# A hybrid decoder layer on one Trainium2 core: small loads moved behind weights and inputs, and GpSimd's work in the dilated attention put in another order

## The chip, the cores and the metric

The kernel runs on one core of one Trainium2 chip. The metric is the device time of one execution in microseconds (us). A core has a matrix engine (TensorE; PE in the profile, its weight loads PEld), VectorE (DVE), ScalarE (ACT), GpSimd (POOL) and SyncE (SP), each with an instruction queue of its own that it works off in order, and 16 DMA engines that move what the queues of SyncE and ScalarE issue.

## The reference, cut to what matters

```python
def hybrid_layer(x, ...):                       # x: 1 x 2048 x 1024, float32
    h = rmsnorm(x, norm_gain)
    proj = h @ w_in                             # 1024 x 2976 columns
    q_a, k_a, v_a, z_a, c_q, c_kv, k_rope, z_b = split(proj)
    # A: 8 heads of 64; three banded patterns (window 128/512/2048, dilation 1/4/16),
    #    mixed by their softmax denominators
    o_a = dilated_window_attention(rmsnorm(q_a), rmsnorm(k_a), v_a, rel_bias)
    # B: 8 heads, low-rank q and kv, rotary key, full causal attention
    o_b = latent_attention(c_q, c_kv, k_rope, positions, ...)
    mixed = concat([o_a * silu(z_a), o_b * silu(z_b)])
    return x + mixed @ w_out
```

## The kernel before, in words

All matrix products that need float32 accuracy are made as three products of two-part operands (`mm3`, line 230: a high part, rounded, and the rest).

**Stage 1, projections (about 0 to 600 us).** The x tiles (128 rows, 512 KB) are loaded by `x_load` (line 194) into three buffers, their square sums are taken (`h0`), they are scaled (`h1`), turned by TensorE and split (`h2`). The weights come in quarters of a column group: `w_load` (line 246) issues two DMAs into one of two buffers `wraw`, `w_split` (line 257) makes the two parts on ScalarE or GpSimd and on VectorE, and at its end issues the load of the quarter after the next one. Column groups run in the order g0, g1, q0, z0, ...; each for the first 8 tiles of rows, then again for the other 8. At the head of the stage (lines 278 to 310) stand, in the text: x tile 0, the norm's gain, a constant matrix CM, two quarters of weights, x tiles 1 and 2, then 14 small loads (positions, the rotary frequencies, gains; each 0.2 to 16 KB), then the splits. `rope_tables` (line 314) needs positions and frequencies; the units of group g1 need its tables and the gain of the rotary key; `up_weights` needs `ugain`; the column gains `gcol` are first used by the units of q0. In this stage the text does not fix the order on an engine: the program is built with `schedule_with_timeline_sim=True` (line 1742), and a scheduler orders the instructions of each queue when the program is built, by a simulation of its own.

**Stage 2, dilated attention (about 600 to 1000 us).** Here the order on every engine is that of the text (`tc.manual_schedule`, line 1544). The loop over `n` (line 1546) goes through 64 units, 8 for each head h (n = 8h + i). In one turn it issues the scores of a head ahead (`groups`: tiles on TensorE, reductions on VectorE, and `q_turn`, GpSimd's casts of Q), the exponentials of the next unit (ScalarE), the transposes and copies of this unit, then the products with V of the unit before (`p_pv`). One third of the third pattern's exponentials is made in one piece: GpSimd subtracts the maximum (line 997), ScalarE takes the exponential (998), VectorE sums (999).

When a head's units are through, its tail follows (`tail`, line 1242): a table from a step (counted from n = 8h + 8) to functions. `a_den0` makes two products on GpSimd (E8 and E32, lines 930 and 937) that TensorE reads in `a_den1` (line 1094), one step later; from them comes the reciprocal of the denominators, which goes through DRAM and comes back broadcast (`a_rd1`). `a_shift` loads the lower half of the accumulator (`bot`) and the gate (`gA_`). `a_sum` (line 1134, GpSimd) adds the halves, `a_gate` (line 1129, VectorE) multiplies gate and reciprocal, `a_out` (line 1139, GpSimd) multiplies both, `a_store` stores. Heads 6 and 7 use `a_outt` (line 1230), with no trip through DRAM. In a turn, step 1 runs ahead of `p_pv`; the other steps are put off behind it:

```python
                    for f in tail(g).get(n - 8 * g - 8, ()):
                        if n - 8 * g - 8 == 1:
                            f()
                        else:
                            late.append(f)
```

From n = 52 on, the loop also does the first pieces of the latent attention (`early`): loads and splits of its keys and queries (`b_split`, lines 1352 and 1353, on GpSimd) and its first scores.

**Stage 3, latent attention (about 1000 to 1340 us), and stage 4, the output product**, follow. The change does not touch their text.

Of the kernel before, what the change touches and what calls it, by code (L numbers as in the profile page):

```python
# [43 lines left out]
B3 = (1,)  # L44
# [57 lines left out]
def hybrid_kernel(ctx: ExitStack, tc: tile.TileContext, x, positions, rel_bias, norm_gain, w_in,  # L102
# [181 lines left out]
    x_load(2)  # L284

    pos_i = P1.tile([NB, 128], I32, name="pos_i")
    sp.dma_start(pos_i, positions.rearrange("o (b p) -> (o b) p", p=128))
    invf = P1.tile([128, 16], F32, name="invf")
    sp.dma_start(invf, bcast_rows(cinv, 16))
    gains = {}  # L290
    for nm, ap, n in (("qr", qr_gain, 32), ("kr", kr_gain, 32)):
        gains[nm] = P1.tile([128, n], F32, name="g_" + nm)
        sp.dma_start(gains[nm], bcast_rows(ap, n))
    ugain = P1.tile([128, 3], F32, name="ugain")
    sp.dma_start(ugain[:, 0:2], q_c_gain.rearrange("o (k p) -> p (o k)", p=128))
    sp.dma_start(ugain[:, 2:3], kv_c_gain.rearrange("o (k p) -> p (o k)", p=128))
    gcol = P1.tile([128, 6], F32, name="gcol")
    dve.memset(gcol, 1.0)
    for i, ap in enumerate((a_q_gain, a_k_gain, qn_gain, kn_gain)):
        src = bass.AP(tensor=ap.tensor, offset=ap.offset, ap=[[1, 64], [1, 1]])  # L300
        sp.dma_start(gcol[0:64, i:i + 1], src)
        sp.dma_start(gcol[64:128, i:i + 1], src)
    for n in range(4):
        w_split(n)
    for b in range(2):
        h0(b)
    dve.scalar_tensor_tensor(gcol[:, 4:5], gcol[:, 0:1], 0.125, gcol[:, 1:2], op0=OP.mult, op1=OP.mult)
    dve.tensor_mul(gcol[:, 5:6], gcol[:, 2:3], gcol[:, 3:4])
    gAcol = gcol[:, 4:5]
    gBcol = gcol[:, 5:6]  # L310

    tabs = {}

    def rope_tables():
# [364 lines left out]
    for gi, (half, nm) in enumerate(seq):  # L679
# [18 lines left out]
        for i, unit in enumerate(units):  # L698
# [8 lines left out]
            if nm == "g0" and half == 1:  # L707
                b = 12 + i
                if i < 1:
                    x_load(b + 3)  # L710
                if i < 2:
                    h0(b + 2)
                if i < 4:
                    h1(b)
                    h2(b)
            clock[0] += 1
            flush()
            main.add(unit)
# [227 lines left out]
    def mid(sel):  # L946
        return sel[:, None, :, None].to_broadcast([128, 4, 4, 4])
# [31 lines left out]
    def m_back2(h):  # L979
# [6 lines left out]
                    2: PP.tile([128, 4, 4], F32, name="d2", bufs=2),  # L986
                    3: PP.tile([128, 16], F32, name="d3", bufs=2)}

    def a_exp(h, w, m, ns=range(4)):
        H = HD[h]  # L990
        if w == 3 and m // 2 in B3:
            if m % 2 == 0 and (h, m) not in exp_done:
                exp_done.add((h, m))
                p = H["P", 3, m // 2].rearrange("p (r s) k -> p r s k", r=2)
                mc = H["mc"].rearrange("p (s r) -> p r s", r=4)[:, m:m + 2, :]
                den = H["den"][3].rearrange("p (s r) -> p r s", r=4)[:, m:m + 2, :]
                pool.tensor_sub(p, p, mc[:, :, :, None].to_broadcast([128, 2, 4, 128]))
                act.activation(p, p, AF.Exp, scale=-1.0)
                H["b3"] = lambda: dve.tensor_reduce(den, p, axis=AX.X, op=OP.add)
            return  # L1000
# [83 lines left out]

    def a_den0(h):
        H = HD[h]
        H["e"] = expand8(H["den"][3], pool), spread(H["den"][2].rearrange("p r n -> p n r")[:, :, None, :].to_broadcast([128, 4, 4, 4]),
                            mid(R32b), "E32", pool)

    def a_den1(h):  # L1090
        H = HD[h]
# [150 lines left out]
    def tail(h):  # L1242
# [5 lines left out]
        if h == 5:  # L1248
# [4 lines left out]
                    7: [lambda: a_out(h, 0), lambda: a_out(h, 1), lambda: a_rd1(h, 2), lambda: a_rd1(h, 3)],  # L1253
                    8: [lambda: a_gate(h, 2), lambda: a_gate(h, 3)],
                    9: [lambda: a_out(h, 2), lambda: a_out(h, 3), lambda: a_store(h)]}
        out = {0: [lambda: a_den0(h)], 1: [lambda: a_den1(h), lambda: a_den2(h)], 2: [lambda: a_rd0(h)],
               3: [lambda: act.dma_start(rD[h], HD[h]["rt"])], 4: [lambda: a_shift(h)],
               5: [lambda: a_rd1(h, 0), lambda: a_rd1(h, 1)], 6: [lambda: a_sum(h, 0), lambda: a_sum(h, 1)],
               7: [lambda: a_gate(h, 0), lambda: a_gate(h, 1), lambda: a_sum(h, 2), lambda: a_sum(h, 3)],
               8: [lambda: a_rd1(h, 2), lambda: a_rd1(h, 3), lambda: a_out(h, 0), lambda: a_out(h, 1)]}  # L1260
        k = 10 if h < 4 else 9
        out[k] = [lambda: a_gate(h, 2), lambda: a_gate(h, 3)]
        out[k + 1] = [lambda: a_out(h, 2), lambda: a_out(h, 3)]
        out.setdefault(12 if h < 4 else 10, []).append(lambda: a_store(h))
        return out

    a_loadb(0)
    a_turnb(0)
# [275 lines left out]
    with tc.manual_schedule(engines={E.PE, E.DVE, E.Activation, E.Pool, E.SP}):  # L1544
        gn = 0
        for n, (h, i) in enumerate(units):
# [29 lines left out]
            for g in (h - 2, h - 1):  # L1576
                if g >= 0:
                    for f in tail(g).get(n - 8 * g - 8, ()):
                        if n - 8 * g - 8 == 1:
                            f()  # L1580
                        else:
                            late.append(f)
# [13 lines left out]
            if n + SLEAD == 55:  # L1596
# [8 lines left out]
                    b_raw(0, "kqk"[u], u // 2)  # L1605
                pre, s0, s1 = b_pre(0), b_blocks_s(0, 0), b_blocks_s(0, 1)
                early = pre[:4] + s0 + pre[4:6] + s1[:4] + pre[6:] + [lambda: b_loadv(0)] + s1[4:]
            if n + SLEAD > 56:
                for f in early[:2]:
                    f()  # L1610
                early = early[2:]
# [135 lines left out]
```

## Time and profile before

| | us |
|---|---|
| median of 3 runs | 1665.05 (1662.9 to 1671.62) |
| the profiled execution | 1660.16 |
| its span, first to last instruction | 1658.3 |
| TensorE busy | 1600.0 (96%) |
| VectorE busy | 969.2 (58%) |
| ScalarE busy | 833.7 (50%) |
| GpSimd busy | 672.1 (41%) |

The profile is one execution. Times in its rows count from the start of the span. In a row of a queue in time order stand start, duration, engine, line, operation, what is written and read, how many instructions the row stands for (x2), and in brackets how long the engine was idle before it and what ended that. A TensorE that is 96% busy has some 58 us without work; and a stretch in which the granted clock is below 1.00 has more that the busy time doesn't show.

### The profile page before, as it was taken

How to read it: one execution, taken by the hardware profiler on the slowest of the kernel's cores; microseconds unless marked ns; L12 is line 12 of the kernel's file. 1: busy time of each engine (PE TensorE's matmuls, PEld its weight loads, DVE VectorE, ACT ScalarE, POOL GpSimd, SP SyncE). 2: the span in 40 equal slices, each digit the busy share in tenths (PEclk: the TensorE clock that was granted, in tenths of full speed). 3: DMA queues.
4: the chain of work that ended last, by engine and by line, in shares of the span. 5: the costliest groups of instructions: out<-in, count | busy, mean ns of one | idle time of the engine just before them, and what ended most of it. 6: DMA issues, size and time to landing. Idle time of an engine off the chain costs nothing.

```text
span 1658.3 us, 29348 instructions
## 1 busy us (share of the span) xinstructions
PE 1600.0 (96%) x10028; PEld 1296.2 (78%) x10028; DVE 969.2 (58%) x2937; ACT 833.7 (50%) x2237; POOL 672.1 (41%) x699
## 2 busy tenths in 40 slices
PE   6999999999999999999999879999999999999998
PEld 5998899989999978888878556666666666567887
DVE  4655564254766334578788576666666666734321
ACT  5655564265656422577778745555555555520000
POOL 2453453014666202135655928565365371421000
PEclk9999999999999999999999899999999999999999
DMA  7347644653465685389785544321321221237642
GB/s 162 103 131 186 166 127 129 180 143 81 123 156 145 186 222 159 107 182 195 180 212 110 138 93 107 82 67 41 73 71 40 70 64 35 74 93 185 183 131 64
DMA packets 237946, 206.97 MB, mean 125 GB/s; under 512 B 108349, under 2 KB 203305, under 8 KB 232164
## 3 DMA queue, kind: packets, MB, share of 16 engines
q1 hardware_dynamic: 150084, 153.86, 37.4%
q10 hardware_dynamic: 87712, 51.24, 11.3%
q8 instruction: 79, 1.29, 0.3%
q14 instruction: 71, 0.58, 0.1%
HBM read 131.21 MB, written 72.25 MB: 123 GB/s over the span
## 4 chain that ended last, share of the span: by engine, by line
PE 83%; DMA 8%; DVE 3%; ACT 2%; POOL 2%; issue 1%; SPq 1%; ACTq 0%; DVEq 0%; POOLq 0%
PE O L1436 9%; PE T L1418 7%; PE mz L231 7%; PE mz L233 7%; PE mz L232 7%; PE S L1393 5%; PE S L1395 4%; PE S L1394 4%; PE S L887 3%; PE po L231 3%; PE po L233 3%; PE po L232 3%; PE O L1068 3%; PE mm L233 3%; PE mm L231 3%; PE mm L232 3%
## 5 line engine op out<-in xcount | busy, mean ns | idle before, releaser
L231 PE MATMUL mz<-wh,hTh 128*128 128x256 f32 (+2 forms) x600 | 182.3, 304 | 1.4 <-ACT hTh L225 1.4
L233 PE MATMUL mz<-wh,hTl 128*128 128x256 f32 (+2 forms) x600 | 178.4, 297 | 2.6 <-DVE hTl L226 2.5
L232 PE MATMUL mz<-wl,hTh 128*128 128x256 f32 (+2 forms) x600 | 177.4, 296 | 0.0
L1423 ACT ACTIVATE ptB<-T 128x512 f32<-128x512 f32 (+3 forms) x160 | 84.5, 528 | 166.8 <-PE T L1418 166.2
L1436 PE MATMUL O<-ptB,VB 128*64 128x512 f32 (+3 forms) x640 | 160.5, 559 | 1.8 <-DVE ptB L1421 1.8
L1411 ACT ACTIVATE P<-P,msB 128x1024 f32<-128x1024 f32 (+4 forms) x104 | 109.4, 1052 | 66.0 <-DVE msB L1398 65.9
L1393 PE MATMUL S<-kBh,qBh 96*128 96x512 f32 (+2 forms) x320 | 133.1, 416 | 0.8 <-DVE msB L1398 0.8
L1393 PEld LDWEIGHTS S<-kBh,qBh 96*128 96x128 f32 x320 | 60.3, 188 | 93.0 <-issue 73.8
L274 DVE SCALAR_TENSOR_TENSOR wl<-wraw,ng,wh 128x256 fp32r<-128x256 f32 (+2 forms) x176 | 85.1, 522 | 76.4 <-ACT wh L273 55.9
L233 PEld LDWEIGHTS mz<-wh,hTl 128*128 128x128 f32 x600 | 115.4, 192 | 3.4 <-DVE hTl L226 2.9
L231 PEld LDWEIGHTS mz<-wh,hTh 128*128 128x128 f32 x600 | 115.1, 192 | 3.6 <-ACT hTh L225 2.3
L1395 PE MATMUL S<-kBh,qBl 96*128 96x512 f32 (+2 forms) x320 | 116.4, 364 | 0.0
L1394 PE MATMUL S<-kBl,qBh 96*128 96x512 f32 (+2 forms) x320 | 116.4, 364 | 0.0
L232 PEld LDWEIGHTS mz<-wl,hTh 128*128 128x128 f32 x600 | 115.4, 192 | 0.2
L147 POOL TENSOR_TENSOR pst<-pst,CM 128x8 f32<-128x8 f32 x48 | 80.1, 1681 | 77.2 <-DVE pst L596 70.7
L1398 DVE CUSTOM_DVE_ANT_0 P<-S,zero 128x512 f32<-128x512 f32 (+1 forms) x96 | 65.1, 678 | 67.5 <-PE S L1395 65.8
L1421 DVE COPY ptB<-T 128x512 f32<-128x512 f32 (+3 forms) x160 | 96.8, 605 | 12.2 <-PE T L1418 11.4
L231 PE MATMUL po<-woh,mh 128*128 128x512 f32 x256 | 100.8, 394 | 2.1 <-ACT woh L1299 1.5
L1418 PE MATMUL T<-CM,P 128*128 128x128 f32 x740 | 99.3, 275 | 2.5 <-DVE gA__12822 L1238 1.2
L232 PE MATMUL po<-wol,mh 128*128 128x512 f32 x256 | 100.4, 392 | 1.1 <-POOL wol L1300 1.1
L233 PE MATMUL po<-woh,ml 128*128 128x512 f32 x256 | 100.2, 392 | 0.0
L273 ACT ACTIVATE wh<-wraw,ng 128x256 fp32r<-128x256 f32 (+2 forms) x168 | 76.9, 514 | 43.4 <-DMA wraw<-in_w_in_dram 20.0
(492 smaller groups left out, 4541.3 us busy)
## 6 DMA issues: line engine op xcount, KB each, us to landing
wraw<-in_w_in_dram SPq DMA_DIRECT2D x72, 256.0 KB
V<-vA SPq DMA_DIRECT2D x24, 512.0 KB
xt<-in_x_dram SPq DMA_DIRECT2D x16, 512.0 KB
GD<-zst ACTq DMA_DIRECT2D x32, 256.0 KB
Q<-qT SPq DMA_DIRECT2D x8, 1024.0 KB
KH<-kT SPq DMA_DIRECT2D x16, 512.0 KB
KL<-kT SPq DMA_DIRECT2D x16, 512.0 KB
mraw<-mixD SPq DMA_DIRECT2D x64, 128.0 KB
```

What stands on the lines that cost most here:

```text
L231: pe.matmul(ps, lh, rh, start=first, stop=False)
L232: pe.matmul(ps, lh, rl, start=False, stop=False)
L233: pe.matmul(ps, ll, rh, start=False, stop=last)
L274: dve.scalar_tensor_tensor(WL[key][:, k, :w], r[:, j, :w], ng[:, k:k + 1], f32(wh), op0=OP.mult, op1=OP.subtract)
L1393: pe.matmul(ps[:, :nm], H["q", "h"][:, q], H["k", "h"][:, k], start=True, stop=False)
L1394: pe.matmul(ps[:, :nm], H["q", "h"][:, q], H["k", "l"][:, k], start=False, stop=False)
L1395: pe.matmul(ps[:, :nm], H["q", "l"][:, q], H["k", "h"][:, k], start=False, stop=True)
L1411: act.activation(t, t, AF.Exp, bias=b, scale=-1.0, accum_out=H["den", c][:, i, d:d + 1])
L1418: pe.transpose(tp[:, d, :], p_part(h, c, d, 128 * j, 128), ident)
L1421: dve.tensor_copy(pt[:, d0:, :], tp[:, d0:, :])
L1423: act.activation(pt[:, d0:, :], tp[:, d0:, :], AF.Copy)
L1436: pe.matmul(o[64 * e:64 * e + 64, d0:, :], V[:, j + e, :], pt[:, d0:, :], start=(j == 0), stop=(j == 4 * c + 2), skip_group_check=True)
```

## The change

In stage 1 six of the small loads go into a function `small_loads`, called in the text at the third tile of group g0, and the eight of `gcol` with the two products made of them into `head_gains`, called at the first tile of g1. In stage 2: the subtraction of line 997 becomes a function `a_less` and is called for heads 6 and 7 at n = 50 and n = 52 (before: when the exponential is issued, n = 53 and n = 61); `a_den0` runs on VectorE for heads 6 and 7, on GpSimd for the others; step 0 of a tail (`a_den0`) now runs ahead of `p_pv`, as step 1 did; and the tables of heads 0 to 4 spread the sums and products otherwise. Cut where a line says "...":

```diff
     pos_i = P1.tile([NB, 128], I32, name="pos_i")
-    sp.dma_start(pos_i, positions.rearrange("o (b p) -> (o b) p", p=128))
     invf = P1.tile([128, 16], F32, name="invf")
-    sp.dma_start(invf, bcast_rows(cinv, 16))
...
+    def small_loads():
+
+        sp.dma_start(pos_i, positions.rearrange("o (b p) -> (o b) p", p=128))
+        sp.dma_start(invf, bcast_rows(cinv, 16))
+        for nm, ap in (("qr", qr_gain), ("kr", kr_gain)):
+            sp.dma_start(gains[nm], bcast_rows(ap, 32))
+        sp.dma_start(ugain[:, 0:2], q_c_gain.rearrange("o (k p) -> p (o k)", p=128))
+        sp.dma_start(ugain[:, 2:3], kv_c_gain.rearrange("o (k p) -> p (o k)", p=128))
+
+    def head_gains():
+        dve.memset(gcol, 1.0)
+        for i, ap in enumerate((a_q_gain, a_k_gain, qn_gain, kn_gain)):
+            src = bass.AP(tensor=ap.tensor, offset=ap.offset, ap=[[1, 64], [1, 1]])
+            sp.dma_start(gcol[0:64, i:i + 1], src)
+            sp.dma_start(gcol[64:128, i:i + 1], src)
+        dve.scalar_tensor_tensor(gcol[:, 4:5], gcol[:, 0:1], 0.125, gcol[:, 1:2], op0=OP.mult, op1=OP.mult)
+        dve.tensor_mul(gcol[:, 5:6], gcol[:, 2:3], gcol[:, 3:4])
+
     for n in range(4):
         w_split(n)
     for b in range(2):
         h0(b)
...
@@ -713,6 +717,10 @@
                     h2(b)
+            if half == 0 and nm == "g0" and i == 2:
+                small_loads()
+            if half == 0 and nm == "g1" and i == 0:
+                head_gains()
             clock[0] += 1
             flush()
             main.add(unit)
@@ -986,15 +994,26 @@
+    less_done = set()
+
+    def a_less(h, m):
+
+        if h in less_done:
+            return
+        less_done.add(h)
+        H = HD[h]
+        p = H["P", 3, m // 2].rearrange("p (r s) k -> p r s k", r=2)
+        mc = H["mc"].rearrange("p (s r) -> p r s", r=4)[:, m:m + 2, :]
+        pool.tensor_sub(p, p, mc[:, :, :, None].to_broadcast([128, 2, 4, 128]))
+
     def a_exp(h, w, m, ns=range(4)):
...
-                pool.tensor_sub(p, p, mc[:, :, :, None].to_broadcast([128, 2, 4, 128]))
+                a_less(h, m)
                 act.activation(p, p, AF.Exp, scale=-1.0)
...
     def a_den0(h):
         H = HD[h]
-        H["e"] = expand8(H["den"][3], pool), spread(H["den"][2]. ...
-                            mid(R32b), "E32", pool)
+        eng = pool if h < 6 else dve
+        H["e"] = expand8(H["den"][3], eng), spread(H["den"][2]. ...
+                            mid(R32b), "E32", eng)
...
-        out = {0: [lambda: a_den0(h)], 1: [lambda: a_den1(h), lambda: a_den2(h)], 2: [lambda: a_rd0(h)],
-               3: [lambda: act.dma_start(rD[h], HD[h]["rt"])], 4: [lambda: a_shift(h)],
-               5: [lambda: a_rd1(h, 0), lambda: a_rd1(h, 1)], 6: [lambda: a_sum(h, 0), lambda: a_sum(h, 1)],
-               7: [lambda: a_gate(h, 0), lambda: a_gate(h, 1), lambda: a_sum(h, 2), lambda: a_sum(h, 3)],
-               8: [lambda: a_rd1(h, 2), lambda: a_rd1(h, 3), lambda: a_out(h, 0), lambda: a_out(h, 1)]}
-        k = 10 if h < 4 else 9
-        out[k] = [lambda: a_gate(h, 2), lambda: a_gate(h, 3)]
-        out[k + 1] = [lambda: a_out(h, 2), lambda: a_out(h, 3)]
-        out.setdefault(12 if h < 4 else 10, []).append(lambda: a_store(h))
-        return out
+        if h == 4:
+            return {0: [lambda: a_den0(h)], 1: [lambda: a_den1(h), lambda: a_den2(h)], 2: [lambda: a_rd0(h)],
+                    3: [lambda: act.dma_start(rD[h], HD[h]["rt"])], 4: [lambda: a_shift(h)],
+                    5: [lambda: a_rd1(h, 0), lambda: a_rd1(h, 1)], 6: [lambda: a_sum(h, 0)],
+                    7: [lambda: a_gate(h, 0), lambda: a_gate(h, 1), lambda: a_sum(h, 1), lambda: a_sum(h, 2)],
+                    8: [lambda: a_rd1(h, 2), lambda: a_rd1(h, 3), lambda: a_out(h, 0), lambda: a_sum(h, 3)],
+                    9: [lambda: a_gate(h, 2), lambda: a_gate(h, 3), lambda: a_out(h, 1)],
+                    10: [lambda: a_out(h, 2), lambda: a_out(h, 3), lambda: a_store(h)]}
+        return {0: [lambda: a_den0(h)], 1: [lambda: a_den1(h), lambda: a_den2(h)], 2: [lambda: a_rd0(h)],
+                3: [lambda: act.dma_start(rD[h], HD[h]["rt"])], 4: [lambda: a_shift(h)],
+                5: [lambda: a_rd1(h, 0), lambda: a_rd1(h, 1)],
+                7: [lambda: a_gate(h, 0), lambda: a_gate(h, 1), lambda: a_sum(h, 0), lambda: a_sum(h, 1)],
+                8: [lambda: a_rd1(h, 2), lambda: a_rd1(h, 3), lambda: a_out(h, 0), lambda: a_sum(h, 2)],
+                9: [lambda: a_out(h, 1), lambda: a_sum(h, 3)], 10: [lambda: a_gate(h, 2), lambda: a_gate(h, 3)],
+                11: [lambda: a_out(h, 2), lambda: a_out(h, 3)], 12: [lambda: a_store(h)]}
...
                     for f in tail(g).get(n - 8 * g - 8, ()):
-                        if n - 8 * g - 8 == 1:
+                        if n - 8 * g - 8 < 2:
                             f()
...
+            if n in (55 - SLEAD, 57 - SLEAD):
+                a_less(6 if n == 55 - SLEAD else 7, 2 * B3[0])
             if n + SLEAD > 56:
```

## Rows read from the trace of the kernel before

**Rows 1.** Busy time by stretch: length, PE, PEld, DVE, ACT, POOL, PEclk, DMA share, GB/s
```profile
0.00:60.00 60.00, 42.80 (x257) 39.53 (x258) 34.02 (x89) 33.18 (x91) 18.22 (x27) 0.94 0.60 138
60.00:360.00 300.00, 299.07 (x1972) 276.33 (x1971) 156.48 (x395) 156.17 (x409) 111.18 (x135) 1.00 0.56 151
...
912.00:1000.00 88.00, 72.47 (x459) 50.44 (x460) 56.40 (x139) 51.79 (x167) 53.68 (x45) 0.90 0.53 118
```

**Rows 2.** DMA busy tenths, 10 to 22 us, 40 slices of 0.3 us
```profile
DMA  9999999969500000000000000000000466998758
```

**Rows 3.** SyncE's queue in time order, first 60 us
```profile
6.46 0.58 SPq L287 DMA_DIRECT2D pos_i<-in_positions_dram  x1
...
11.52 0.51 SPq L301 DMA_DIRECT2D gcol<-in_a_q_gain_dram  x1
...
17.64 0.59 SPq L302 DMA_DIRECT2D gcol<-in_kn_gain_dram  x1
18.33 0.53 SPq L253 DMA_DIRECT2D wraw<-in_w_in_dram  x1
...
23.71 0.58 SPq L362 DMA_DIRECT2D relm<-in_rel_bias_dram  x1
```

**Rows 4.** VectorE in time order, first 50 us
```profile
9.16 1.93 DVE L274 SCALAR_TENSOR_TENSOR wl<-wraw,ng,wh 128x320 fp32r<-128x320 f32 x4
...
14.10 0.26 DVE L319 CAST pt<-pos_i 16x128 f32<-16x128 int32 x1 [2.33 <-DMA pos_i<-in_positions_dram]
```

**Rows 5.** TensorE's waits from 680 to 912 us: total, times, longest
```profile
PE S L1094 <- POOL E L930: 3.6, 3, 1.7
PE S L887 <- DVE m L899: 2.5, 2, 2.1
PE S L887 <- POOL Q L826: 2.0, 2, 1.0
```

**Rows 6.** TensorE's waits from 912 to 1000 us
```profile
PE T L1035 <- ACT PT L1045: 4.3, 1, 4.3
PE S L1094 <- POOL E L930: 3.3, 1, 3.3
```

**Rows 7.** ScalarE in time order, 912 to 1000 us
```profile
923.52 1.06 ACT L998 ACTIVATE P<-P 128x1024 f32<-128x1024 f32 x1 [4.68 <-POOL P L997]
```

**Rows 8.** GpSimd in time order, the tail of head 1
```profile
783.75 2.50 POOL L1134 TENSOR_TENSOR bot<-acc,bot 64x512 f32<-64x512 f32 x2 [7.04 <-DMA bot<-acc]
...
791.84 2.50 POOL L1139 TENSOR_TENSOR bot<-bot,gA__10126 64x512 f32<-64x512 f32 x2
794.29 0.41 POOL L930 TENSOR_TENSOR E<-d,CM 128x128 f32<-128x128 f32 x1
...
800.11 0.33 POOL L937 TENSOR_TENSOR E<-m,CM 128x64 f32<-128x64 f32 x1 [4.47 <-PE T L1031]
```

**Rows 9.** TensorE in time order, 790 to 830 us
```profile
794.75 0.39 PE L1094 MATMUL S<-CM,E 128*128 128x16 f32 x2 [1.72 <-POOL E L930]
```

**Rows 10.** Busy time by stretch, behind that wait (columns as rows 1)
```profile
796.00:800.00 4.00, 4.00 (x23) 3.62 (x20) 2.70 (x16) 1.08 (x3) 0.00 (x0) 0.58 1.27 235
```

**Rows 11.** Line 1129, the gate products of head 1: ns min/median/max
```profile
L1129 DVE TENSOR_TENSOR gA__10126<-rbA,gA__10126 x4: 675/883/1121, 786.2 to 801.8; 64x512 f32<-64x512 f32 x4
```

**Rows 12.** GpSimd in time order, 910 to 925 us
```profile
913.07 0.40 POOL L930 TENSOR_TENSOR E<-mc,CM 128x128 f32<-128x128 f32 x1 [3.30 <-PE O L1068]
...
915.97 1.49 POOL L1352 TENSOR_SCALAR kBh<-qkraw 96x512 fp32r<-96x512 f32 x1 [2.24 <-DMA qkraw<-kN]
...
921.58 1.91 POOL L997 TENSOR_TENSOR P<-P,mc 128x1024 f32<-128x1024 f32 x1
```

**Rows 13.** SyncE's queue in time order, 940 to 956 us
```profile
946.29 0.47 SPq L1142 DMA_DIRECT2D mixD<-bot  x1
```

**Rows 14.** VectorE in time order, 912 to 1000 us
```profile
961.42 0.68 DVE L1238 TENSOR_TENSOR gA__12589<-T,gA__12589 64x512 f32<-64x512 f32 x1 [1.38 <-DMA gA__12589<-GD]
```

**Rows 15.** Line 943, the nearest shape to E32 on VectorE
```profile
L943 DVE TENSOR_TENSOR pk<-S,CM x16: 203/216/225, 658.9 to 975.8; 128x64 f32<-128x64 f32 x16
```

More of the change, by code (lines that the diff above doesn't have):

```diff
@@ L286, in hybrid_kernel @@
     pos_i = P1.tile([NB, 128], I32, name="pos_i")
-    sp.dma_start(pos_i, positions.rearrange("o (b p) -> (o b) p", p=128))
     invf = P1.tile([128, 16], F32, name="invf")
-    sp.dma_start(invf, bcast_rows(cinv, 16))
[L290 to L293, printed above, removed]
+    gains = {nm: P1.tile([128, 32], F32, name="g_" + nm) for nm in ("qr", "kr")}
     ugain = P1.tile([128, 3], F32, name="ugain")
-    sp.dma_start(ugain[:, 0:2], q_c_gain.rearrange("o (k p) -> p (o k)", p=128))
-    sp.dma_start(ugain[:, 2:3], kv_c_gain.rearrange("o (k p) -> p (o k)", p=128))
     gcol = P1.tile([128, 6], F32, name="gcol")
[L298 to L302, printed above, removed]
+    gAcol = gcol[:, 4:5]
+    gBcol = gcol[:, 5:6]
+    def small_loads():
[13 more added lines that the diff above has]
+        dve.tensor_mul(gcol[:, 5:6], gcol[:, 2:3], gcol[:, 3:4])
     for n in range(4):
@@ L306, in hybrid_kernel @@
         h0(b)
[L307 to L310, printed above, removed]
     tabs = {}
@@ L994, in a_exp @@
                 p = H["P", 3, m // 2].rearrange("p (r s) k -> p r s k", r=2)
-                mc = H["mc"].rearrange("p (s r) -> p r s", r=4)[:, m:m + 2, :]
                 den = H["den"][3].rearrange("p (s r) -> p r s", r=4)[:, m:m + 2, :]
-                pool.tensor_sub(p, p, mc[:, :, :, None].to_broadcast([128, 2, 4, 128]))
+                a_less(h, m)
                 act.activation(p, p, AF.Exp, scale=-1.0)
@@ L1086, in a_den0 @@
         H = HD[h]
-        H["e"] = expand8(H["den"][3], pool), spread(H["den"][2].rearrange("p r n -> p n r")[:, :, None, :].to_broadcast([128, 4, 4, 4]),
-                            mid(R32b), "E32", pool)
+        eng = pool if h < 6 else dve
+        H["e"] = expand8(H["den"][3], eng), spread(H["den"][2].rearrange("p r n -> p n r")[:, :, None, :].to_broadcast([128, 4, 4, 4]),
+                            mid(R32b), "E32", eng)
     def a_den1(h):
```

## Prediction, made before the change was run

> **What bounds the kernel now.** I read the views in this order: busy time by stage, then for each stage in which TensorE has gaps, who released it, then the queue of that releaser. By stage [rows 1], TensorE is busy 299.07 of 300 us from 60 to 360, and has gaps in the first 60 us (42.80 busy) and from 912 to 1000 (72.47 of 88). So a microsecond won at the start is not lost again in the projections behind it, since nothing there makes TensorE wait; and the change has to earn its time at the start and in the dilated attention.
>
> At the start, the strip of the 16 DMA engines from 10 to 22 us [rows 2] is 40 slices of 0.3 us: the engines are nearly full until slice 11 and idle in the 20 behind it, 13.3 to 19.3 us, that is 6.0 us. SyncE's queue shows why [rows 3]: from 6.46 to 17.64 it issues the 14 small loads. The eight of gcol alone take from 11.52 to 18.2, 6.7 us where eight times 0.59 would be 4.7: the queue also stands, for transfers of x to end. The third quarter of the weights is issued only at 18.33. Its buffer was free long before: VectorE has ended the four splits of the first two quarters at 9.16 + 1.93 = 11.1 us [rows 4]. VectorE too stands for a small load, 2.33 us for pos_i at 14.10 [rows 4], with the row statistics of the next x tile queued behind.
>
> In the attention the lists of TensorE's waits name GpSimd: to 912 us [rows 5] 3.6 us for E in three waits and 2.0 for Q in two, behind it [rows 6] 3.3 for E in one. They also name ScalarE once, 4.3 us [rows 6]. That one is GpSimd too: ScalarE had itself waited 4.68 us for the subtraction of line 997 [rows 7].
>
> **The change part by part.**
>
> *Small loads.* The weights and x tiles 3 to 5 are moved ahead of 14 issues. In this stage a scheduler, not the text, orders each queue: the load of relm, whose text is in the middle of the second group, stands at 23.71, ahead of the rest of the first [rows 3]. So some of the six loads of small_loads may still fill a gap behind x tile 2; the third quarter's weights are then issued at 10 to 12 us all the same. What limits then is the DMA: it is full to 13.3, so the weights follow there and not at 19.3. Gain: at most the 6.0 idle us; 5.5 taken, since the 14 small loads still cost some DMA time. The stall of 2.33 us on VectorE lies inside these 6 us and is not counted again. From below: the moved loads cost SyncE 14 issues of about 0.6 us [rows 3], 8 us, but behind x tile 5 the DMA is still draining megabytes, which hides them. If that cover is gone, they delay weights and x one for one: 5.5 less 8 is 2.5 us lost. Range -2.5 to +6.
>
> *E of the denominators first (a_den0), sums a step later, heads 0 to 3.* Read GpSimd's queue for head 1 [rows 8]. It waits 7.04 us for the transfer of bot to 783.75, does two sums (2.50), then two of the Q casts that TensorE needs (one of the two waits for Q, 1.0 us [rows 5]), two more sums, two casts, two products (2.50), and only then E at 794.29, for which TensorE waits 1.72 [rows 9]. After the change the casts of step 7 stand ahead of the first sums, and E stands behind two sums and two casts only: about 783.75 + 2.5 + 1.6 = 788 against 794.3, while TensorE came for it at 793.0. So that wait is covered by 5 us. The same pattern comes back for head 3, and in small for head 2. Removed: the three waits for E, 3.6 us, and the two for Q, 2.0 [rows 5], 5.6 in all. Behind the E waits the granted clock is low: mean 0.58 in 796 to 800 [rows 10], part of it at the 1.2 GHz level, so 4 x 0.42 = 1.7 us of work are lost, twice: 3.4. Sum 9.0. What is late next: VectorE. The gate products of step 7 stay where they are and take up to 1.1 us each there instead of 0.7 [rows 11], and the score reductions are queued behind them. So of the two Q waits I keep half (1.0) and of the clock some 2.4: 3.6 + 1.0 + 2.4 = 7. Range 3 to 9. The products and sums put off to steps 8 and 9 cost nothing: GpSimd is idle there for some 4.5 us per head (4.47 before 800.11 [rows 8]), and no engine waits for bot before the store at step 12, which is not moved. Head 4's own table moves three sums and one product by one step; TensorE has no wait for GpSimd there, so nothing.
>
> *The subtraction of heads 6 and 7 earlier (a_less).* It takes 1.91 us [rows 12]. At 921.58 it stands behind four splits of the latent attention; ScalarE waits 4.68 for it and TensorE 4.3 [rows 6, 7]. Earlier, it fits where GpSimd is idle (3.30 us before the E at 913.07 for head 6, 2.24 before 915.97 for head 7 [rows 12]), so it costs nothing there. TensorE's 4.3 us go. But they are not all kept: from 915.97 on GpSimd's queue is never empty until its last products of head 5 release the store at 946.29 [rows 13]. Behind that store stand the loads of V, bot and gA for the last heads, and VectorE waits for gA until 961.42 [rows 14], TensorE behind it. GpSimd is shorter by 1.91 and, with head 6's E gone to VectorE, by 0.7: 2.6 us. So 2.6 of the 4.3 are kept, more if the second load of V, which waits for TensorE, comes earlier too. Taken 2.5, range 0 (a longer stall at gA, with the low clock behind it) to 6.
>
> *a_den0 of heads 6 and 7 on VectorE.* Head 7: TensorE waits 3.3 us for E [rows 6], because E follows the last product on GpSimd. On VectorE it follows the sum ahead of that product. No row has these shapes on VectorE; the nearest is 128x64 at 216 ns [rows 15], the 128x128 on GpSimd takes 0.41 us [rows 8]. So 0.5 us for both (0.4 to 0.8), and a gain of 0.5, range -1 to 2.
>
> A rule bears on these two moves. The row: the gate product has a minimum of 675 ns and a maximum of 1121 [rows 11], the longer ones beside GpSimd. The Trainium skill, "SBUF — State Buffer", section "Who interferes with whom", says that a VectorE instruction with two SBUF inputs and a GpSimd instruction that reads SBUF exclude each other for the whole instruction. By it the two E products, which read den and CM, could each wait for one split or product on GpSimd. The trace agrees in direction, up to 0.45 us on one gate product. By the rule in full the last part is a loss, which is a rival below.
>
> **Sum.** 5.5 + 7 + 2.5 + 0.5 = 15.5 us. The profiled execution took 1660.16 us (span 1658.3, 1.9 around it) and lies 4.9 below the median of the three runs, 1665.05, so I take the difference off the median: 1649.5. By parts the low end is -2.5 + 3 + 0 - 1 = -0.5, the high end 6 + 9 + 6 + 2 = 23.
>
> **Rivals.**
> *VectorE becomes the attention's bound.* For: its reductions stand behind two gate products of up to 1.1 us each; TensorE waits 2.5 us for m of line 899 already [rows 5]. Against: it still has gaps where TensorE waits for E. Then the attention gives some 2 us, the start 5.5: 1657.5.
> *The scheduler leaves the weights where they were, or SyncE stands again for x's transfers*, so that the change does not do at the start what its text says. For: the order is not the text's. Against: the 14 issues alone hold the queue from 6.46 to 17.64. Then only the attention gains, 10 us: 1655.
> *Lock between VectorE and GpSimd.* The two E products on VectorE each wait for a GpSimd instruction of 1.3 to 1.9 us (the sizes in [rows 8, 12]), TensorE behind them, and the end's 3 us are used up: 15.5 - 3 = 12.5, so 1652.5. That is what the rule of the Trainium skill ("SBUF — State Buffer", "Who interferes with whom") gives if taken in full. The trace bears it out in part only.
> *All covered by other waits:* 1665.
> *Slower: SyncE's queue in the first group.* Its small loads come between x tile 5 and the stores of v; 14 issues are 8 us, VectorE's cast of pos_i then waits in order for its load, with the splits of h behind it, as it did for 2.33 us [rows 4]. TensorE loses those 8 us and works at the low level behind them, another 4 (at half speed over as long, as in part in [rows 10]), and the second group's weights, in the same queue, come later by the same: in place of a gain of 5.5 a loss of 12 or more. It decides from a wait of about 18 us on, since the attention's 10 us must be used up and 8 more be lost: some 1675.
>
> **How the numbers follow.** Forecast 1649.5, chance 0.47, own range 1642 to 1657; lock 0.10; VectorE's bound 0.16; start without gain 0.14; all covered 0.07; slower 0.06. A measurement of this kernel tells about 0.5%, 8.3 us, from no change: faster is below 1656.7, slower above 1673.4. Faster: 0.45 of the forecast, 0.08 of the lock, 0.04 and 0.07 of the next two: 0.64. Slower: 0.06. The same: 0.30. The range goes from 1641 (forecast's upper gains) to 1663, which leaves out the slow case, most of "all covered", and a little of the forecast's tail.
>
> **What would show it.** The start: the third quarter's weights issued before 13 us, no idle DMA from 13 to 19, TensorE's first 60 us busy for 46 or more. The attention: no wait of line 1094 for E, none for Q; GpSimd's subtraction of heads 6 and 7 before its splits; ScalarE's 4.68 gone; the store now at 946.29 some 2.6 us nearer to the split at its left. Wrong would be: DMA idle for other waits of SyncE, waits for m of line 899 in place of those for E and Q, or a wait at gA several times the 1.38 us of [rows 14].

## The result, and the profile after

The changed kernel takes 1648.91 us (median of 4 runs, 1644.64 to 1650.31) against 1664.33 (median of 4, 1662.9 to 1671.62): ratio 0.9898, 95% interval 0.9876 to 0.9919, which is 17.0 us less (13.5 to 20.6). The ratio is not that of the two medians, which stand 15.4 us apart. The forecast was 1649.5. The profiled execution took 1650.31 us and its span is 1648.5, 9.8 less than the 1658.3 of before; why the two profiles stand closer than the medians is worked out below.

In the kernel after, the lines have moved: 1094 (`a_den1`) is 1114, 930 and 937 (the E products) are 938 and 945, 1134 (`a_sum`) is 1154, 1129 (`a_gate`) is 1149, 1139 (`a_out`) is 1159, 997 (the subtraction) is 1007, 899 is 907.

**By stage** (columns as in rows 1; the last row is of before, for the stretch that rows 1 leave out):

```profile
0.00:60.00 60.00, 47.29 (x308) 45.23 (x309) 35.73 (x94) 36.18 (x100) 18.46 (x27) 0.97 0.65 145
60.00:360.00 300.00, 298.06 (x1954) 275.45 (x1952) 155.57 (x393) 153.68 (x404) 113.26 (x136) 0.99 0.56 153
680.00:912.00 232.00, 228.38 (x1932) 196.22 (x1931) 187.60 (x894) 176.88 (x611) 126.90 (x156) 0.99 0.82 179
912.00:1000.00 88.00, 76.94 (x455) 53.77 (x454) 64.11 (x153) 47.31 (x141) 47.82 (x37) 0.88 0.54 112
```

```profile
680.00:912.00 232.00, 222.16 (x1869) 192.25 (x1871) 188.78 (x894) 166.85 (x576) 114.46 (x146) 0.99 0.77 172
```

TensorE is busy 4.5 us more in the first 60 (47.29, before 42.80), 6.2 more from 680 to 912 (228.38, before 222.16) and 4.5 more in the last stretch (76.94, before 72.47).

**The start.** First the DMA strip from 10 to 22 us, as in rows 2; then SyncE's queue, as in rows 3.

```profile
DMA  9999999999999999773999079989212599800889
```

```profile
6.62 0.58 SPq L296 DMA_DIRECT2D pos_i<-in_positions_dram  x1
...
10.36 0.38 SPq L253 DMA_DIRECT2D wraw<-in_w_in_dram  x1
...
14.43 0.55 SPq L196 DMA_DIRECT2D xt<-in_x_dram  x1
...
16.16 0.51 SPq L307 DMA_DIRECT2D gcol<-in_a_q_gain_dram  x1
```

The 20 idle slices of [rows 2] are busy now, 6.8 tenths on the mean. The third quarter of the weights is issued at 10.36 instead of 18.33 [rows 3]. The scheduler still put four of the six small loads into the gap behind x tile 2 (pos_i at 6.62); two loads of `ugain` and the first of `gcol` now follow the weights and x tile 3 (issued at 14.43, before at 20.50). VectorE still stands for `pos_i` as in [rows 4], 2.27 us where it was 2.33. TensorE's waits in the first 60 us name the x tiles, scaled, turned and split (lines 211, 225 and 226): 17.1 us in all before, 11.6 after (9.3 and 9.5 of them for the first tile). A wait of 1.2 us for the split of the weights is new.

**The dilated attention.** TensorE's waits from 680 to 912 us, all of 0.3 us and more (releaser, total, times, longest):

```profile
PE S L922 <- DVE m L907: 1.4, 1, 1.4
PE T L1054 <- DVE PT L1062: 0.7, 1, 0.7
PE S L895 <- DVE m L907: 0.3, 1, 0.3
```

E and Q of [rows 5] are not in it. GpSimd's tail of head 1 shows why (compare rows 8):

```profile
780.83 2.51 POOL L1154 TENSOR_TENSOR bot<-acc,bot 64x512 f32<-64x512 f32 x2 [4.73 <-DMA bot<-acc]
783.29 0.61 POOL L836 CAST Q<-Q 128x512 fp32r<-128x512 f32 x1
783.85 1.07 POOL L834 CAST Q<-Q 128x512 fp32r<-128x512 f32 x1
784.89 0.91 POOL L938 TENSOR_TENSOR E<-d,CM 128x128 f32<-128x128 f32 x1
785.76 0.32 POOL L945 TENSOR_TENSOR E<-d,CM 128x64 f32<-128x64 f32 x1
```

E stands 4.06 us behind the first sum (before 10.54) and both products are there at 786.1; TensorE comes for them at 789.36. From 789 to 793 us, around that point, its granted clock is 1.00, with 32 matmuls where the 4 us of [rows 10] had 23 at a mean of 0.58:

```profile
789.00:793.00 4.00, 3.89 (x32) 3.08 (x30) 3.84 (x26) 2.88 (x10) 2.39 (x3) 1.00 1.18 296
```

**The turn to the latent attention.** GpSimd's two subtractions and its first split, then ScalarE's exponential, then SyncE's store (the rows that answer rows 12, 7 and 13).

```profile
898.41 1.90 POOL L1007 TENSOR_TENSOR P<-P,mc 128x1024 f32<-128x1024 f32 x1
...
902.35 1.91 POOL L1007 TENSOR_TENSOR Pr<-Pr,mc 128x1024 f32<-128x1024 f32 x1
904.76 1.49 POOL L1377 TENSOR_SCALAR kBh<-qkraw 96x512 fp32r<-96x512 f32 x1 [0.49 <-DMA qkraw<-kN]
```

```profile
907.39 1.06 ACT L1017 ACTIVATE P<-P 128x1024 f32<-128x1024 f32 x1
```

```profile
932.56 0.47 SPq L1162 DMA_DIRECT2D mixD<-bot  x1
```

Both subtractions are ahead of the splits, ScalarE no longer waits for one, and the store is 27.80 us behind the first split where it was 30.32 [rows 12, 13]. TensorE's waits from 902 to 1000 us, all of 1 us and more:

```profile
PE S L1114 <- DVE E L938: 3.1, 1, 3.1
PE T L1054 <- DVE gA__12590 L1258: 2.6, 1, 2.6
PE T L1050 <- ACT Pr L1039: 1.6, 2, 1.5
PE T L1054 <- DVE PT L1062: 1.5, 2, 0.7
PE T L1443 <- DVE gA__12822 L1258: 1.2, 1, 1.2
```

The 4.3 us for PT of [rows 6] are gone; the last wait for E has changed its engine and hardly its size (3.3 to 3.1). The longest wait for gA, 2.3 us before, is 2.6.

### The profile page after: what moved, and what is told of

It is laid out like the page before. It is cut to its first block, busy times and chain, and to the rows that moved or that the text cites. A ratio compares the mean times of both kernels' runs of the same rounds, so it can differ in the third digit from the quotient of the medians.

```text
span 1648.5 us, 29342 instructions
## 1 busy us (share of the span) xinstructions
PE 1601.6 (97%) x10028; PEld 1300.1 (79%) x10028; DVE 969.4 (59%) x2941; ACT 833.4 (51%) x2237; POOL 673.7 (41%) x695
## 4 chain that ended last, share of the span: by engine, by line
PE 84%; DMA 7%; DVE 3%; ACT 3%; issue 1%; SPq 0%; POOL 0%; ACTq 0%; DVEq 0%; POOLq 0%
PE O L1461 9%; PE T L1443 7%; PE mz L231 7%; PE mz L232 7%; PE mz L233 7%; PE S L1418 5%; PE S L1419 4%; PE S L1420 4%; PE S L895 3%; PE po L231 3%; PE po L233 3%; PE po L232 3%; PE O L1087 3%; PE mm L232 3%; PE mm L233 3%; PE mm L231 3%
```

## Marks that allow traces to be compared

Fixed windows show different work once a kernel is ahead, so the experiments are read by marks: the times at which TensorE begins the same matmul. Mark A is head 0's first matmul of `a_den1`, B head 7's backward step (line 984, before 976), C and D the `a_den1` of heads 6 and 7. F lies some 34 us behind D, in the latent attention: the third transpose of `rdB` (line 1479, before 1454). These are the rows of after, and then B to D of before:

```profile
723.10 0.29 PE L1114 MATMUL S<-CM,E 128*128 128x16 f32 x2
...
904.91 0.29 PE L984 MATMUL S<-CM,E 128*128 128x16 f32 x2
...
923.01 0.29 PE L1114 MATMUL S<-CM,E 128*128 128x16 f32 x2
...
961.72 0.40 PE L1114 MATMUL S<-CM,E 128*128 128x16 f32 x2 [3.09 <-DVE E L938]
...
996.13 0.27 PE L1479 MATMUL T<-CM,rdB 128*4 128x128 f32 x1
```

```profile
916.33 0.45 PE L976 MATMUL S<-CM,E 128*128 128x16 f32 x2
...
939.47 0.29 PE L1094 MATMUL S<-CM,E 128*128 128x16 f32 x2
...
974.67 0.61 PE L1094 MATMUL S<-CM,E 128*128 128x16 f32 x2 [3.31 <-POOL E L930]
```

The same marks of all profiles, in us. "Won" is the ratio's distance from 1 times the median of the runs of before taken beside it, with its interval:

| kernel | A | A to B | B to C | B to D | B to F | won in the time of a run |
|---|---|---|---|---|---|---|
| before | 726.08 | 190.25 | 23.14 | 58.34 | 91.83 | |
| e1_loads | 722.53 | 189.82 | 23.23 | 59.34 | 92.73 | 5.0 (2.8 to 7.2) |
| e8_gcol | 721.80 | 190.60 | 23.41 | 59.40 | 93.81 | 4.5 (1.7 to 7.3) |
| e6_first | 725.16 | 184.57 | 23.25 | 58.87 | 92.43 | 3.0 (0 to 6.0) |
| e7_table | 726.33 | 185.82 | 23.20 | 59.47 | 94.57 | 8.0 (5.0 to 10.8) |
| e3_tail | 726.64 | 180.95 | 23.17 | 58.87 | 92.14 | 9.0 (5.8 to 12.0) |
| e4_less | 728.20 | 188.26 | 19.94 | 57.28 | 90.50 | 1.2 (-1.3 to 3.7) |
| e2_attn | 723.76 | 181.85 | 20.01 | 56.49 | 91.61 | 9.0 (5.5 to 12.5) |
| after | 723.10 | 181.81 | 18.10 | 56.81 | 91.22 | 17.0 (13.5 to 20.6) |
| e5_nodve | 719.65 | 180.69 | 20.16 | 58.69 | 92.04 | 16.2 (13.0 to 19.5) |
| e9_den7 | 719.81 | 182.78 | 20.48 | 53.60 | 91.00 | 16.8 (13.2 to 20.3) |
| e10_vfirst | 718.71 | 181.47 | 17.94 | 54.06 | 89.05 | 20.5 (16.5 to 24.5) |
| e11_both | 721.95 | 181.27 | 21.20 | 54.27 | 91.36 | 19.5 (15.3 to 23.7) |

A moves by some 4 us between executions of the same stage 1 (723.8 to 728.2 with the loads of before, 718.7 to 723.1 with those of after), so single traces don't size the start. A to B and B to D are steadier, but not exact: e4, whose edit acts only just ahead of B, has 188.26 where the other three with the middle as before have 189.8 to 190.6. B to F takes 91.8 to 94.6 in the six traces whose turn to the latent attention is as before, so there less than a us or two is not told from chance.

## Experiments

**e1_loads: the kernel before, with the small loads moved and nothing else.**

```diff
+    def small_loads(): ...
+    def head_gains(): ...
...
+            if half == 0 and nm == "g0" and i == 2:
+                small_loads()
+            if half == 0 and nm == "g1" and i == 0:
+                head_gains()
```

> Only the small loads are moved; the attention is as before. Theory (the DMA engines idled 6.0 us because the third quarter of the weights was issued late, and nothing in the projections behind makes TensorE wait): 3 to 5.5 us faster than before, the third quarter issued before 13 us, TensorE 46 to 48 us busy in the first 60, and the same lead of 3 us or more still there when head 0's E product starts (721.1 before). Rival (the lead is given back by waits in the later projections, since another order is built for the whole stage): 0 to 2 us.

Measured: 1661.32 us against 1667.51, ratio 0.9970 (0.9957 to 0.9983). A is at 722.53, the rest as before. So the start is worth about 5 us (at least 2.8), and the rival that the lead is given back later falls. The third quarter's weights are issued at 9.94, so the prediction's rival that the scheduler leaves them where they were falls too.

**e8_gcol: of these, only the eight loads of `gcol` moved.** The other six stay at the head of the queue.

```diff
-    for i, ap in enumerate((a_q_gain, a_k_gain, qn_gain, kn_gain)): ...
+    def head_gains(): ...
...
+            if half == 0 and nm == "g1" and i == 0:
+                head_gains()
```

> The kernel before, with the eight loads of gcol and the two products made of them moved to the first tile of g1; the other six small loads stay at the head of the queue. The run with all 14 loads moved had left four of the six in their gap at 6.6 to 8.6 us anyway. Theory: the eight loads of gcol, which stand for transfers of x, alone hold SyncE's queue from 11.52 to 18.2 us, so this run issues the third quarter of the weights by 12.5 us, shows no idle DMA from 13 to 19, and gains the same as all 14: TensorE busy 46.5 or more of the first 60 us, the median 3 to 6 us below the kernel before. Rival: the six hold it as well, the weights come at 14 us or later, and the first 60 us show under 45 busy.

Measured: 1661.55 against 1666.66, ratio 0.9973 (0.9956 to 0.9990). SyncE's queue and the first 60 us:

```profile
9.22 0.47 SPq L296 DMA_DIRECT2D ugain<-in_kv_c_gain_dram  x1
11.59 0.38 SPq L253 DMA_DIRECT2D wraw<-in_w_in_dram  x1
14.15 0.38 SPq L255 DMA_DIRECT2D wraw<-in_w_in_dram  x1
```

```profile
0.00:60.00 60.00, 45.75 (x297) 43.73 (x298) 34.59 (x92) 34.66 (x96) 18.39 (x27) 0.97 0.66 145
```

The first half of the third quarter is issued at 11.59 behind all six small loads, the second at 14.15 (before 18.33 and 18.91), and the gain is that of e1 within the interval. TensorE's 45.75 lies between the two cases' bounds (46.5 and 45), so a us of it may be the six loads'. The queue's waits for transfers of x stay: before, it stands 1.9 us at each of the first two loads of `gcol`, and here 1.8 and 2.2 us at the two weight loads themselves. What went is the eight issues ahead of the weights and of x tile 3, with the DMA idle behind them: from 10 to 22 us the DMA now moves 2.25 MB, before 1.10.

**e2_attn: the whole attention part without the loads.** All of the diff ahead of the prediction from `a_less` on; cut:

```diff
+    def a_less(h, m): ...
...
+        eng = pool if h < 6 else dve
...
-                        if n - 8 * g - 8 == 1:
+                        if n - 8 * g - 8 < 2:
```

> Only the attention part of the change; stage 1 is as before, in the same order. Theory: 9 to 12 us faster; the waits for E and Q gone up to the last head, which still waits about 3 us. Rival (VectorE is the bound, so the waits come back as waits for m of line 899's counterpart): 2 to 5 us faster.

Measured: 1657.57, ratio 0.9946 (0.9925 to 0.9967): 9.0 us. With e1's 5.0 that is 14.0; the whole change gives 17.0 (13.5 to 20.6). Within these intervals the two parts add up.

**e3_tail: the tables of heads 0 to 4 and step 0 ahead of `p_pv`; no `a_less`, E all on GpSimd.**

```diff
-        out = {0: [lambda: a_den0(h)], ...
+        if h == 4:
+            return {0: [lambda: a_den0(h)], ...
...
-                        if n - 8 * g - 8 == 1:
+                        if n - 8 * g - 8 < 2:
```

> Of the attention part only the new tables of heads 0 to 4 and step 0 ahead of the products; a_den0 stays on GpSimd for all heads and the subtraction stays where it was. Theory: 7 to 8.5 us faster, all of it before head 6 (the time between head 0's E and head 7's scores' back step shorter by that), and the 4.3 us wait of heads 6 and 7 still there. Rival (these waits are covered by VectorE's): 3 us or less.

Measured: 1658.06, ratio 0.9946 (0.9928 to 0.9965). A to B is 180.95, as short as with the whole change; B to D is 58.87, as before. The middle's gain is all here, and the wait of 4.3 us of [rows 6] is still there. In time e3 wins as much as e2 (9.0 both), so the run times don't show what the rest of e2 adds.

**e6_first and e7_table: the two halves of e3, each alone.** First the one line:

```diff
-                        if n - 8 * g - 8 == 1:
+                        if n - 8 * g - 8 < 2:
```

> The kernel before, with one edit: step 0 of every tail (a_den0, the two E products) runs ahead of p_pv and so ahead of the products of the head before it; the old tables stay. It asks which half of the middle's gain is this line's. Theory: in GpSimd's queue E stands before the two products of 2.50 us together but still behind all four sums and the casts, so for head 2 at about 791.8 instead of 794.29; TensorE comes for it at about 793. The three waits for E before 912 us (3.6 us) go, with the low clock behind them (3.4 by the working of the prediction); the two waits for Q (2.0) stay. From the first denominators of head 0 to the last backward step of head 7 TensorE needs 190.25 us before and 181.8 with the whole change; here some 184. Rival: the tables carry the gain, since the sums ahead of E are what makes it late; then waits for E of 1 us or more stay and the stretch is 188 or longer. In the median the theory gives some 1659 to 1661, the rival 1663 or more.

Then the tables alone:

```diff
-        out = {0: [lambda: a_den0(h)], ...
+        if h == 4:
+            return {0: [lambda: a_den0(h)], ...
```

> The kernel before, with the new tables of heads 0 to 4 alone; step 0 stays behind p_pv. Theory: the casts of Q now stand ahead of the sums, so the two waits for Q go (2.0 us and what the clock loses behind them). E of the next head stands behind two sums, the casts, one product and a third sum: 783.75 + 2.5 + 1.6 + 2.5 = 790.4 and the p_pv copies, if any, so it too is ahead of TensorE's 793 and most of the waits for E go. The stretch from the first denominators of head 0 to the last backward step of head 7 comes to some 183 us (before 190.25, the whole change 181.8). Rival: E stays late without the line that runs step 0 ahead; then the list of TensorE's waits still names E for 2 us or more before 912, and the stretch is 187 or longer.

Measured: e6 1663.31 against 1666.66, ratio 0.9982 (0.9964 to 1.0000); e7 1658.48, ratio 0.9952 (0.9935 to 0.9970). The waits from 680 to 912 us, first of e6, then of e7:

```profile
PE S L887 <- POOL Q L826: 2.5, 2, 2.0
PE S L887 <- DVE m L899: 2.1, 1, 2.1
PE S L914 <- DVE m L899: 1.4, 1, 1.4
```

```profile
PE S L914 <- DVE m L899: 4.7, 3, 2.1
PE S L887 <- DVE m L899: 2.1, 1, 2.1
```

e6 does what its theory said: E gone, Q left, A to B 184.57 for "some 184". In e7 both are gone, so either edit alone is enough for E, and my rival for e7 falls; but the stretch is 185.82 and not 183, because VectorE's maxima are waited for. Of the totals, 2.1 us here and 2.5 before lie at 680 to 685 us, ahead of A; behind A it is 4.7 us in three waits, before 1.4 in one. That is the wait the prediction feared for the whole change, and it is there only without the line that runs step 0 ahead (behind A: e6 1.4, e3 0.4, after 1.4). The gate products ahead of the first of those maxima, in e7 and in after, and TensorE's wait behind them in e7:

```profile
787.53 2.96 DVE L1129 TENSOR_TENSOR gA__10126<-rbA,gA__10126 64x512 f32<-64x512 f32 x2 [1.15 <-DMA gA__10126<-GD]
```

```profile
783.63 1.91 DVE L1149 TENSOR_TENSOR gA__10126<-rbA,gA__10126 64x512 f32<-64x512 f32 x2 [0.25 <-DMA gA__10126<-GD]
```

```profile
791.33 0.37 PE L914 MATMUL S<-KH,Q 128*128 128x256 f32 x1 [2.05 <-DVE m L899]
```

Counted from A, the pair of e7 starts 0.7 us later than that of after (it waits 1.15 us for its load) and takes 1.05 us more. Apart the halves shorten A to B by 5.7 and 4.4, together by 9.3. By the medians e7 is ahead of e6, by the stretch e6 of e7; the intervals overlap, and which half is worth more stays open.

**e4_less: the subtraction earlier, and nothing else.**

```diff
+            if n in (55 - SLEAD, 57 - SLEAD):
+                a_less(6 if n == 55 - SLEAD else 7, 2 * B3[0])
```

> Only the subtraction of heads 6 and 7 is moved ahead. Theory (what TensorE wins behind it, 4.3 us and some clock, is mostly given back at the wait for gA, whose load stands behind a store that GpSimd's products release, and GpSimd's queue is only 1.9 us shorter): 1.5 to 3 us faster, with a wait at line 1238 for gA that is longer than the 1.38 us of before. Rival (all is kept): 5 to 6.5 us faster. Other rival (nothing, for the low clock behind the longer wait): 0.

Measured: 1664.87, ratio 0.9993 (0.9978 to 1.0008), not told from zero. The marks say more: B to C is 19.94 instead of 23.14, but B to D only 57.28 instead of 58.34. Of 3.2 us won at head 6, 1.1 are left at head 7 (1.8 against the mean of the six traces with the turn as before). The interval excludes the rival that all is kept (5 us or more), not the one of no gain.

**e5_nodve: the whole change, with E of heads 6 and 7 on GpSimd.**

```diff
-        eng = pool if h < 6 else dve
+        eng = pool
```

> The whole change, but with a_den0 of heads 6 and 7 left on GpSimd. Theory (the move to VectorE is worth little: E's two products take 1.5 to 2.0 us on VectorE beside GpSimd in the changed kernel, and the last head's wait is 3.1 us against 3.3): 0 to 1.5 us slower than the whole change, at head 6's E (den1) up to 1 us later, the last head's wait 3 to 3.6 us. Rival (VectorE is the worse place, by the exclusive lock of the Trainium skill, page SBUF - State Buffer, section Who interferes with whom): 1 to 3 us faster than the whole change.

Measured: 1649.73 against 1665.75, ratio 0.9903 (0.9883 to 0.9922): 0.8 us less won than with the whole change, far inside the interval. In the waits, E of heads 6 and 7:

```profile
PE S L1114 <- POOL E L938: 4.1, 2, 3.3
```

So the other engine spares 0.8 us at head 6 (4.1 - 3.3) and 0.2 at head 7 (3.3 to 3.1). In the marks it is 1.9 at D (58.69 for 56.81) and 0.8 at F. The rival, that VectorE is the worse place, has nothing for it here, but the interval alone does not exclude it.

**e9_den7: the last wait for E taken away.** On the kernel after, head 7's E is made on GpSimd at n = 63, ahead of the last tails.

```diff
+            if n == 63:
+                a_den0(7)
```

> The whole change, and a_den0 of head 7 is issued one turn earlier (n = 63, ahead of that turn's products), on GpSimd, which waits for VectorE there anyway. Theory (TensorE's last wait for E, 3.1 us, and the low clock behind it, some 7 us near 0.5, come from the place of a_den0 in the queue alone): the wait is gone, and the turn to the latent attention is 4 to 6 us earlier than in the whole change. Rival (TensorE only waits for the next thing, the load of gA for head 7 or VectorE's copies): 0 to 2 us.

Measured: 1649.51, ratio 0.9899 (0.9878 to 0.9921), no better than after. No wait for E is left and D comes 3.2 us earlier (B to D 53.60 for 56.81), but the largest entry from 902 to 1000 us is now a new one, its 3.7 us behind D:

```profile
PE S L1418 <- DVE msB L1423: 5.3, 2, 3.7
```

The same wait makes 0.2 us in all of after. B to F is 91.00, in after 91.22: of the 3.2 us at D 0.2 are left at F. They are given back to VectorE's first score maxima of the latent attention. The rival had the size right (0 to 2 us), though it named the load of gA or VectorE's copies as the next wait.

**e10_vfirst: head 7's second loads of V ahead of head 5's store.** On the kernel after:

```diff
+            if n == 57:
+                a_loadv(7, 2)
+                a_loadv(7, 3)
...
-            if i == 1 and h:
+            if i == 1 and 0 < h < 7:
```

> The whole change, and SyncE issues the two late loads of V for head 7 ahead of head 5's store instead of behind it. Theory (the wait for gA of head 6, 2.6 us, hangs on the chain last products on GpSimd, store, V, bot, gA; the DMA is nearly idle before the store): the V loads are issued some 3 us earlier, gA lands 2 to 4 us earlier, the wait at line 1258 falls below 1 us, and 1.5 to 3 us are won. Rival (the V loads wait for TensorE to leave the buffers of head 6, and the store waits behind them): no gain or a loss of 1 to 2 us.

Measured: 1647.15, ratio 0.9877 (0.9853 to 0.9901). The wait at gA, which had grown to 2.6, is

```profile
PE T L1054 <- DVE gA__12590 L1258: 1.1, 1, 1.1
```

and B to D is 54.06, 2.8 us shorter than in after. At F 2.2 of them are still there (89.05 for 91.22), unlike in e9. By its median this is the fastest kernel here, 1.8 us below after, but against its own runs of before the two intervals overlap widely: a better version, or none, can't be said.

**e11_both: e9 and e10 in one**, on the kernel after.

```diff
+            if n == 57:
+                a_loadv(7, 2)
+                a_loadv(7, 3)
...
+            if n == 63:
+                a_den0(7)
```

> The two edits of the runs beside it together. Theory (two waits one behind the other, each with its own cause): the sum of both, 5 to 9 us faster than the whole change, some 22 us faster than the kernel before. Rival (one wait hides the other): no better than the better of the two.

Measured: 1647.59, ratio 0.9883 (0.9858 to 0.9908). B to D is 54.27 and B to F 91.36, no shorter than in after. msB is waited for 6.0 us in two waits. The two don't add up: VectorE's msB is what is late next.

## Why the prediction was right, and where not

*The size.* Means of the marks over all traces that hold a part give the terms. Start: A is 726.03 over the six with the loads as they were (before, e2, e3, e4, e6, e7) and 720.96 over the six with all of them moved (after, e1, e5, e9, e10, e11): 5.1. Middle, A to B: 190.2 over before, e1 and e8, 181.5 over the seven with tables and step 0 changed (e2, e3, after, e5, e9, e10, e11): 8.7 (8.2 with e4 in the first group). The turn, B to D: 59.05 over the six without `a_less` (before, e1, e8, e3, e6, e7), 56.65 over e2 and after: 2.4. At F of this 1.5 is left (92.9 to 91.4), no more than the spread there. Sum 16.2 at D and 15.3 at F; predicted 15.5; medians 15.4 apart. That it is so near is partly luck, since the middle gave more than was said and the turn less.

*Start, 5.5 taken, 5.1 found.* The signs came: the weights before 13 us, the DMA at 6.8 tenths in the 20 slices that were idle (one of them still is), TensorE's first 60 us at 47.29 (46 wanted). The reason given, that the queue and not the DMA's rate held weights and x, is shown by e8; that the eight of `gcol` would do it alone I had not seen. Which of the two carries the gain, the weights or x tile 3, no run separates; TensorE's waits name x. One reading was wrong: VectorE's 2.33 us for `pos_i` end at 14.10, so most of them lie ahead of the idle 13.3 to 19.3, and they are still there. A us or two goes where the prediction saw nothing to lose: behind the start, TensorE now waits once 1.6 to 2.0 us for a copy of q (line 521) between 120 and 240 us, in all six traces with all the loads moved, 1.8 in e8, and at most 0.7 with the loads as they were; 60 to 360 us is busy 298.06 for 299.07. "Not lost again in the projections" was nearly right.

*Middle, 7 taken, 8.7 found.* The mechanism is the predicted one: E behind two sums and two casts, Q's casts ahead of the other sums, the low clock behind the waits gone. The mis-sized term is the cut from 9.0 to 7 for VectorE as the next bound. It didn't become one: behind A the waits for m are one of 1.4 us before and one of 1.4 after. The 2.5 us of [rows 5] from which the step argued lie ahead of A and of every tail, and so say nothing of what is late next in the tails:

```profile
682.03 0.36 PE L887 MATMUL S<-KH,Q 128*128 128x256 f32 x1 [2.05 <-DVE m L899]
```

Why the maxima come in time stays open in part. In after the gate products of step 7 are shorter than before (head 1's pair 1.91 for 2.14, head 2's 1.42 for 3.55), but in e3, with A to B as short, head 1's pair takes 2.28. e7 shows the feared case, with the tables alone.

*The subtraction, 2.5 taken.* The account, that 4.3 us of wait go and 2.6 are kept because the store hangs on the same chain on GpSimd, held up to the store (2.5 nearer). In marks: 3 to 5 us won at C, 2.4 at D with E's move, 1.1 with `a_less` alone (e4) and 0.4 in e5, which has it with E on GpSimd (58.69 for 59.05). So this is the term that was taken too high: with E's 0.5 the turn was to give 3.0 and gave 2.4 at D and 1.5 at F. Some of it went to gA, whose wait grew from 2.3 to 2.6, as the low end had it. By time alone this step is not shown: e4's interval takes in zero, and e2 wins no more than e3.

*E of heads 6 and 7 on VectorE, 0.5 taken.* The gain is of the order that was said (0.8 and 0.2 in the waits, 0.8 at F), for another reason: it is mostly at head 6, and the gain was expected at head 7. The two products take not 0.5 us but 2.0 for head 6 and 0.96 for head 7 (below), and the wait at head 7 stays, because E stands where it did in VectorE's order, behind the last turn's work.

*The rivals.* VectorE as bound: seen in e7, not in the change. Scheduler: the weights moved. Covered: excluded by the interval. SyncE's queue in the first group: TensorE has no wait for positions or gains, and VectorE's for `pos_i` is as before, since four of those loads stay at the queue's head. Lock: seen in the rows of E, which take 1.5 and 0.5 us longer than the 0.5 costed, but the 3 us of loss did not come: without the move (e5) the kernel is not shown to be faster.

*Why the profiles differ by 9.8 only.* At A after is 3.0 ahead (the latest A of the six with its start), at D 13.0, at the first product of the output stage 12.2, at the end 9.8. The output stage, by its first and last start, in before and in after:

```profile
L231 PE MATMUL po<-woh,mh x256: 388/393/504, 1472.6 to 1653.0; 128*128 128x512 f32 x128
```

```profile
L231 PE MATMUL po<-woh,mh x256: 389/393/628, 1460.4 to 1643.2; 128*128 128x512 f32 x128
```

180.4 and 182.8 us. Over the thirteen profiles it takes 182.3 to 185.3, but for the profile of before, which has the shortest. No text of that stage changed. So the profiled execution of before was short in a place that the change doesn't touch, which accounts for part of its 4.9 us below the median.

## What to carry to other kernels

Read a stall of the bound engine back along the queue of its releaser, and ask which instructions ahead of the awaited one nobody waits for: here it was eight loads of 0.25 KB ahead of weights and a tile of x of 512 KB, and sums ahead of two products of 0.4 us. Before cutting a gain because another engine is "next", check that the waits for that engine lie in the stretch that the change touches (here 2.5 of 3.9 us lay ahead of it); and near a change of stage look behind the next wait before counting what a removed one gives (3.2 won and 1.1 kept one head later in e4; 3.2 won and 0.2 kept some 35 us later in e9; 2.8 won and 2.2 kept in e10).

## What the runs showed of the hardware that was not expected

Products of both engines took longer when VectorE and GpSimd multiplied from SBUF at once, and the small ones took up to five times as long (246 to 1289 ns). E's rows, first of before, then of after (shortest, median, longest in ns, first and last start):

```profile
L930 POOL TENSOR_TENSOR E<-d,CM x8: 395/400/413, 721.1 to 974.2; 128x128 f32<-128x128 f32 x8
```

```profile
L938 POOL TENSOR_TENSOR E<-d,CM x6: 405/846/910, 718.1 to 884.9; 128x128 f32<-128x128 f32 x6
L938 DVE TENSOR_TENSOR E<-d,CM x2: 710/710/710, 919.7 to 961.0; 128x128 f32<-128x128 f32 x2
L945 DVE TENSOR_TENSOR E<-d,CM x2: 246/768/1289, 920.3 to 961.6; 128x64 f32<-128x64 f32 x2
```

On GpSimd the four products of d that stand beside VectorE's gate products take 0.84 to 0.91 us (one is 784.89, beside 783.63 to 785.54); the two that don't, at 718.13 and 818.30, take 0.41, and the product of m, which never does, 396 to 412 ns. On VectorE the 128x64 product takes 1289 ns at 920.34, beside the second of GpSimd's sums (two from 919.00, 2.54 us), and 246 at 961.59, when GpSimd's last product has ended (960.26, 1.26 us). The Trainium skill ("SBUF — State Buffer", "Who interferes with whom") has a VectorE instruction with two SBUF inputs contend with a GpSimd instruction that reads SBUF, under an exclusive lock; these rows agree, in both directions. That the overlap is the cause is read from the times and was not tried by a run of its own. On GpSimd it cost TensorE nothing here, since the products of heads 0 to 5 still came before it.
